# A hybrid decoder block on one core: six shared temporary tiles for the attention stage, the gate's sigmoid in place, forget gate and token sums by turns, attention heads stored by ScalarE

## The chip, the cores and the metric

The kernel runs on one core of a Trainium2 chip. A core has five engines, and each works through a queue of instructions of its own in program order: TensorE (PE, matrix products, with its weight loads listed apart as PEld), VectorE (DVE), ScalarE (ACT), GpSimd (POOL) and SyncE (SP). SP computes nothing; most transfers between device memory and the on-chip memory are issued from its queue, some from POOL's, and after the change some from ScalarE's. Engines wait for each other and for transfers by semaphores. The metric is the device time of one launch in microseconds (us), as the median of several runs. The kernel is written with a layer that tracks which tile is written and read by whom, and that places the waits.

## The reference

One layer of a decoder for 512 tokens of width 2048, all in float32. The token mixer has two groups of heads behind one input projection; both outputs are concatenated and go through one output projection `w_o`. A gated feed-forward stage with a short convolution follows. Cut to the stage that the change touches:

```python
proj = h @ w_in            # columns: gq, gk, gv, gg, ga, dq, dk, dv
log_a = log_sigmoid(ga @ w_alpha_up + b_alpha) / GLA_TAU          # forget gate, rank 16
o_a = gla_chunked(gq, gk, gv, log_a)                              # 4 heads, 128 keys, 256 values
o_a = rmsnorm(o_a, gla_norm) * silu(gg)                           # silu(g) = g * sigmoid(g)
lam = exp(sum(lambda_q1 * lambda_k1)) - exp(sum(lambda_q2 * lambda_k2)) + lambda_init
# diff_attention, 4 heads, causal, in query blocks of 128:
p = softmax(q k^T * scale + alibi)                                # for two halves, p1 and p2
o_b = rmsnorm((p1 - lam * p2) @ v, diff_norm) * (1 - lambda_init)
m = concatenate([o_a, o_b]) @ w_o
x = x + rmsnorm(m, attn_post_norm)
# then the feed-forward part
```

## The kernel before

**Products in halves.** Every float32 operand of a large product is split into a rounded high part and the rest: ScalarE copies the high part (L137 for weights, L150 for activations), VectorE subtracts it (L138, L151), and PE makes three products, high by high, low by high, high by low. The split weights go through a ring of three slots (`ring`), so PE can be two slots behind the splits and no more. The activations lie in `ah` and `al` for the whole stage.

**The input projection in units.** Most of the 6,160 columns of `w_in` are done in units of 512 columns (class `InUnit`), each by seven block products instead of eight. The seven segments are called x0, z0, y0, z1, x1, y1 and y2; each has two ring slots of 24 products with 256 columns (L743 to L745). Four of them use sums of token blocks, `s5`, `s2`, `s3` and `s7`, which `first_sums` and `last_sums` make beforehand out of `ah` and `al` (VectorE L404 to L425, then split). A segment adds up in a bank of the product memory; a bank that is used for a second term must be copied out first (L754, L759, L768, L790 on ScalarE, L773, L779 and L784 on VectorE). So L759 copies z0's bank (tile `u11`), and z1, which runs with `s3` in the same bank, waits for that.

**Background work.** The attention itself is not a stage of its own. It is written as generators in a list `fill`; after each ring slot `step()` advances the first generator in the list by a share that `pace` sets. First come `forget_gate`, `first_sums` and `last_sums`, one after the other, under the first projections; then `gla_heads` and `diff_heads` under the units. The order of instructions in each engine's queue is then set by a list scheduler with a cost model, within the limits of the tiles and banks; the first 52 us, and some blocks far behind this stage, are placed by hand.

**What the generators do.** `forget_gate` loads the 16 columns of `ga` (tile `gar`), splits them into `gas` (columns 0 to 15 high, 64 to 79 low, zeros between), makes 32 products with 80 columns of weights by 512 tokens (L446, L447), copies the result (L449), makes four more products (L457) and takes -|z| through exp and ln in two wide tiles `za` of 1024 columns (L459 to L465), then a prefix sum (L470). `gla_head` does seven levels a head, each with a product (L522) that VectorE merges under a mask (L525) and with the factor tile `qe` (L513). `diff_heads` works in query blocks: two score products (L614), softmax (exp on ScalarE L622, scaling L629, difference on VectorE L630), four stages behind each other: the probabilities are turned by PE (L637) and copied (L639), multiplied with the values (L646), normalized (L649, L652), turned again (L659), copied into a `dst` tile (L661) and stored to device memory through SP's queue (L662, which the profile lists under the helper's line L48).

**The end of the stage.** The last two of ten units are those of the gate. As each quarter of a gate unit comes out, `done` loads the matching part of the GLA output (`op`), takes the sigmoid into a tile `sg` (L811), multiplies (L812, L813) and, for the first unit, stores to `ogd`. Then `place_diff` loads the stored heads (`dt`) and `turn_gate` loads `ogd` (`ogt`) and turns the blocks on PE (L825), so that `ah` and `al` hold the mixer's output, which `w_o` multiplies (L191 to L193).

**Tiles.** The stage's temporaries come from rings of buffers by tag: `tmp` (four of 2 KB a partition), `quarter` (three of 1 KB), `wide` (two of 4 KB), `qk` (four), `ub` (five). A ring hands out its buffers in turn, and a new tile waits until the last use of the one that had its buffer.

Of the kernel before, what the change touches and what calls it, by code (L numbers as in the profile page):

```python
# [9 lines left out]
F32 = mybir.dt.float32  # L10
# [25 lines left out]
def hybrid_layer(ctx: ExitStack, tc: tile.TileContext, x, attn_pre_norm, w_in, w_alpha_up, b_alpha,  # L36
# [112 lines left out]
    def split(hi, lo, src):  # L149
        act(hi, src, AF.Copy)  # L150
        tt(lo, src, hi.bitcast(F32), ALU.subtract)  # L151
# [195 lines left out]
    for li, hs in enumerate(LEVELS):  # L347
        nb = 64 // hs
        m = quarter("m")[:, :64]
# [13 lines left out]
    lp = quarter("lp").rearrange("p (a d) -> p a d", a=2)  # L363
# [9 lines left out]
    cols = few.tile([P, 4 + 4 * NF], F32, name="cols")  # L373
    rows = tmp("rows")[:NF, :].rearrange("p (a d) -> p a d", a=4)
    ba = quarter("ba")[:4, :P]
# [8 lines left out]
    nc.vector.tensor_copy(cols, cb[:, :4 + 4 * NF])  # L384
# [44 lines left out]
    def forget_gate():  # L429
        gar = quarter("gar").rearrange("p (k r) -> p k r", r=RANK)  # L430
        dma(gar, w_in3[:, :, C_GA:C_GA + RANK])
        gas = mx.tile([P, KT, 80], F32R, name="gas", tag="v", bufs=1)
        nc.gpsimd.memset(gas.bitcast(F32), 0.0)
        split(gas[:, :, 0:RANK], gas[:, :, 64:64 + RANK], gar)
        wup = block_tile("wup")[:80, :]
        nc.gpsimd.memset(wup, 0.0)
        dma(wup[0:RANK, :], w_alpha_up[0])
        dma(wup[64:64 + RANK, :], w_alpha_up[0])
# [5 lines left out]
        gav = gab[:80, :].rearrange("p (t c) -> p t c", c=P)  # L444
# [3 lines left out]
        gaT = block_tile("gaT")[:80, :]  # L448
        nc.vector.tensor_copy(gaT, gab[:80, :])  # L449
# [44 lines left out]
    def gla_head(h, q, k, b, got, fetch):  # L494
        e0 = (h % 2) * GDV
        room = mx.tile([P, NT * GDV + 256], F32, name="gvt", tag="v", bufs=1)
        vt, ec = room[:, :NT * GDV].rearrange("p (t e) -> p t e", t=NT), room[:, NT * GDV:NT * GDV + 4]
# [5 lines left out]
        def prepare(hs):  # L503
# [8 lines left out]
            qe = quarter("qe")  # L512
# [19 lines left out]
        nxt = prepare(LEVELS[0])  # L532
        yield
        for li, hs in enumerate(LEVELS):
            cur = nxt
            if li + 1 < len(LEVELS):
                nxt = prepare(LEVELS[li + 1])
# [20 lines left out]
        st = None  # L558
        for c in range(4):
# [12 lines left out]
            if c < 3:  # L572
                pk = bank()
                mm(pk[:, :GDV], kT[:, c * P:(c + 1) * P], vc, start=True, stop=True)
                ns = quarter("st")
# [10 lines left out]
    def diff_heads():  # L586
# [68 lines left out]
        def store(n, on):  # L655
# [6 lines left out]
            dma(dstd[h][:, :, qb * P:(qb + 1) * P], o.rearrange("p (j c) -> p j c", j=2))  # L662
# [33 lines left out]
    class InUnit:  # L696
        count = 0

        def __init__(self, turned, cols, done):
# [935 lines left out]
```

## Time and profile before

| | |
|---|---|
| median of 3 runs | 2121.33 us (2121.28 to 2121.49) |
| profiled execution | 2118.62 us, span 2116.9 us |
| busy in the span: PE / DVE / ACT / POOL | 2067.5 / 1535.6 / 981.3 / 283.3 us |
| transfers | 358.60 MB, mean 169 GB/s |
| granted TensorE clock, mean | 0.994 |

Times in the trace are counted from the start of the span. Up to 52 us the first projections run in an order by hand; the forget gate and the token sums lie between 52 and 160 us, the GLA heads from there to about 425 us and the attention heads from about 440 to 612 us; `w_o` starts in earnest at 640 us. PE is busy nearly throughout, so a change can win only where PE waits or where its clock is lowered, and lose wherever it makes PE wait. In lists of waits a row names the engine and line that waited, then who released it, then the total, the number of times and the longest. In rows of single instructions the bracket at the end gives the idle time of that engine ahead of the instruction and what ended it. In tables by stretch of time each engine has its busy time and its number of instructions; PEclk is the clock that was granted to TensorE, as a share of full speed.

### The profile page before, as it was taken

Reading aid. Unit: us, or ns where it says so; the run is one execution under the profiler, and the core shown is the slowest. Engines: PE = TensorE matmul, PEld = TensorE weight load, DVE = VectorE, ACT = ScalarE, POOL = GpSimd, SP = SyncE. Lnnn points to the kernel's source line nnn. Section 1 sums busy time; section 2 is a strip of 40 time slices with the busy share of each in tenths; the row PEclk is TensorE's granted clock in tenths of the full one; section 3 lists DMA queues with packets and bytes.
Section 4 is the critical chain, followed back from the end, with each engine's and each line's share of the span. In section 5 each row is a group of like instructions: output and inputs, shape, how many; then the busy total and the mean of one; then the engine's idle time right before and its main releaser. Section 6 shows DMA issues by size and latency. Waiting matters only on the chain.

```text
span 2116.9 us, 35567 instructions
## 1 busy us (share of the span) xinstructions
PE 2067.5 (98%) x14449; PEld 1908.2 (90%) x14449; DVE 1535.6 (73%) x1844; ACT 981.3 (46%) x1264; POOL 283.3 (13%) x306
## 2 busy tenths in 40 slices
PE   7999999999979999999999999999999999999998
PEld 6789999999878889899999999999999878887886
DVE  5596776666763246887786777877877868888887
ACT  4454444455652234353544544454444554444443
POOL 0112222222200000001111111111110111110100
PEclk9999999999989999999999999999999999999999
DMA  5469878888754344457757667577567777676653
GB/s 208 144 151 199 196 167 186 180 198 201 170 179 169 100 157 161 120 120 172 172 129 192 151 145 192 141 174 175 140 164 186 212 230 180 173 195 168 168 168 141
DMA packets 280696, 358.60 MB, mean 169 GB/s; under 512 B 14592, under 2 KB 221876, under 8 KB 278612
## 3 DMA queue, kind: packets, MB, share of 16 engines
q1 hardware_dynamic: 195732, 261.95, 36.5%
q0 software_dynamic: 84800, 94.38, 29.3%
q8 instruction: 113, 1.85, 0.3%
q14 instruction: 51, 0.42, 0.1%
HBM read 311.72 MB, written 44.56 MB: 168 GB/s over the span
## 4 chain that ended last, share of the span: by engine, by line
PE 48%; issue 41%; POOL 3%; DVE 3%; DMA 3%; ACT 1%; POOLq 0%; SPq 0%; DVEq 0%; ACTq 0%
PE bank L192 3%; PE bank L193 3%; PE bank L191 3%; PE bank L739 3%; PE bank L741 3%; PE bank L740 3%; PE bank L743 3%; PE bank L745 3%; PE bank L744 3%; PE bank L1217 2%; PE bank L1216 2%; PE bank L1215 2%; PE bank L175 2%; PE bank L174 2%; PE bank L173 2%
## 5 line engine op out<-in xcount | busy, mean ns | idle before, releaser
L137 ACT ACTIVATE ring<-raw 128x1024 fp32r<-128x1024 f32 x315 | 333.2, 1060 | 523.8 <-PE bank L1216 113.1
L138 DVE TENSOR_TENSOR ring<-raw,ring 128x1024 fp32r<-128x1024 f32 x315 | 383.9, 1221 | 243.2 <-ACT ring L137 241.2
L1217 PE MATMUL bank<-ah,ring 128*128 128x256 f32 x1280 | 354.1, 277 | 1.7 <-DVE ring L138 1.7
L1215 PE MATMUL bank<-ah,ring 128*128 128x256 f32 x1280 | 353.4, 276 | 0.0
L1216 PE MATMUL bank<-al,ring 128*128 128x256 f32 x1280 | 353.4, 276 | 0.0
L137 ACT ACTIVATE ring<-rt 128x1024 fp32r<-128x1024 f32 x221 | 233.2, 1059 | 223.1 <-PE bank L1216 139.6
L138 DVE TENSOR_TENSOR ring<-rt,ring 128x1024 fp32r<-128x1024 f32 x221 | 269.0, 1221 | 89.4 <-ACT ring L137 87.3
L1217 PEld LDWEIGHTS bank<-ah,ring 128*128 128x128 f32 x1280 | 240.2, 188 | 3.0 <-DVE ring L138 3.0
L1215 PEld LDWEIGHTS bank<-ah,ring 128*128 128x128 f32 x1280 | 240.3, 188 | 0.1
L1216 PEld LDWEIGHTS bank<-al,ring 128*128 128x128 f32 x1280 | 240.2, 188 | 0.1
L1318 PE MATMUL bank<-ring,ah 128*128 128x512 f32 x424 | 166.5, 393 | 4.2 <-DVE ring L138 4.2
L1319 PE MATMUL bank<-ring,al 128*128 128x512 f32 x424 | 165.1, 389 | 0.0
L1317 PE MATMUL bank<-ring,ah 128*128 128x512 f32 x424 | 158.3, 391 | 1.5 <-ACT ring L137 1.0
L192 PE MATMUL bank<-ring,ah 128*128 128x512 f32 x280 | 109.8, 393 | 0.0
L191 PE MATMUL bank<-ring,ah 128*128 128x512 f32 x280 | 109.7, 396 | 0.1
L193 PE MATMUL bank<-ring,al 128*128 128x512 f32 x280 | 109.6, 394 | 0.0
L1163 POOL DMA_DIRECT2D raw<-in_w_ffn_in_dram x40 | 50.9, 1274 | 406.5 <-DVE ring L138 403.5
L1318 PEld LDWEIGHTS bank<-ring,ah 128*128 128x128 f32 x424 | 79.6, 188 | 24.8 <-DVE ring L138 8.7
L743 PE MATMUL bank<-ring,ah 128*128 128x256 f32 x320 | 93.6, 293 | 4.3 <-DVE u L784 1.9
L1317 PEld LDWEIGHTS bank<-ring,ah 128*128 128x128 f32 x424 | 79.4, 188 | 20.0 <-ACT ring L137 3.0
L1319 PEld LDWEIGHTS bank<-ring,al 128*128 128x128 f32 x424 | 79.6, 188 | 16.3
L1163 POOL DMA_DIRECT2D rt<-in_w_ffn_in_dram x40 | 51.0, 1280 | 321.1 <-DVE ring L138 242.9
(349 smaller groups left out, 5691.1 us busy)
## 6 DMA issues: line engine op xcount, KB each, us to landing
raw<-in_w_ffn_in_dram SPq DMA_DIRECT2D x96, 512.0 KB, 5.9
raw<-in_w_in_dram SPq DMA_DIRECT2D x56, 512.0 KB, 5.2
raw<-in_w_ffn_out_dram SPq DMA_DIRECT2D x48, 512.0 KB, 6.4
raw<-in_w_in_dram POOLq DMA_DIRECT2D x40, 512.0 KB, 6.8
rt<-in_w_ffn_in_dram SPq DMA_DIRECT2D x40, 512.0 KB, 6.2
rt<-in_w_ffn_in_dram POOLq DMA_DIRECT2D x40, 512.0 KB, 6.0
raw<-in_w_ffn_in_dram POOLq DMA_DIRECT2D x40, 512.0 KB, 7.3
raw<-in_w_o_dram SPq DMA_DIRECT2D x32, 512.0 KB, 3.7
```

The lines of the kernel that those rows point to most:

```text
L137: act(hi, raw, AF.Copy)
L138: tt(lo, raw, hi.bitcast(F32), ALU.subtract)
L191: mm(banks[t], ah[:, t, s, :], w[0][:, k, :], start=st, stop=False)
L192: mm(banks[t], ah[:, t, s, :], w[1][:, k, :], start=False, stop=False)
L193: mm(banks[t], al[:, t, s, :], w[0][:, k, :], start=False, stop=sp)
L743: mm(o, sh[:, n, kk, :], wh[:, k, :], start=st, stop=False, **NOW)
L1215: mm(o, wh, sh[:, :, kk, :], start=start and kk == 0 and n == 0, stop=False, **NOW)
L1216: mm(o, wh, sl[:, :, kk, :], start=False, stop=False, **NOW)
L1217: mm(o, wl, sh[:, :, kk, :], start=False, stop=kk == HK - 1, **NOW)
L1317: mm(b[j], sh[:, o:o + P], w[0][:, q, :], start=start and st == 0, stop=False, **NOW)
L1318: mm(b[j], sh[:, o:o + P], w[1][:, q, :], start=False, stop=False, **NOW)
L1319: mm(b[j], sl[:, o:o + P], w[0][:, q, :], start=False, stop=st == 3, **NOW)
```

## The change

Six things are changed at once.

- The ring `tmp` grows from four to six buffers, and the ring `quarter` goes; what used it (mask `m`, `lp`, `ba`, `gar`) takes a `tmp` tile. In a GLA head `qe` now alternates between the two halves of one `tmp` tile, so it has two buffers instead of three, and the state `st` does the same. The on-chip memory used stays the same.
- `gas` has 48 columns instead of 80, the low part at 32.
- `za` is four `qk` tiles of 512 columns instead of two wide ones; exp and ln run on four tiles, with a pause of the generator between them. The wide tiles are then free for the token sums.
- `forget_gate` and the token sums are advanced by turns instead of one after the other.
- In a gate unit a hook `before` loads `op` ahead of the last segment of a quarter; `done` multiplies `op` by u first (VectorE), takes the sigmoid in place on u (ScalarE), and multiplies. There is no tile `sg`.
- The 16 stores of `dst` are issued by ScalarE's queue.

```diff
     def tmp(name):
-        return mx.tile([P, S], F32, name=name, tag="tmp", bufs=4)
-
-    def quarter(name):
-        return mx.tile([P, 256], F32, name=name, tag="w1", bufs=3)
...
-        m = quarter("m")[:, :64]
+        m = tmp("m")[:, :64]
...
-    lp = quarter("lp").rearrange("p (a d) -> p a d", a=2)
+    lp = tmp("lp")[:, :256].rearrange("p (a d) -> p a d", a=2)
...
+    ec = cols[:, 4 + 4 * NF:]
     rows = tmp("rows")[:NF, :].rearrange("p (a d) -> p a d", a=4)
-    ba = quarter("ba")[:4, :P]
+    ba = tmp("ba")[:4, :P]
...
     def forget_gate():
-        gar = quarter("gar").rearrange("p (k r) -> p k r", r=RANK)
+        gar = tmp("gar")[:, :KT * RANK].rearrange("p (k r) -> p k r", r=RANK)
         dma(gar, w_in3[:, :, C_GA:C_GA + RANK])
-        gas = mx.tile([P, KT, 80], F32R, name="gas", tag="v", bufs=1)
+        gas = mx.tile([P, KT, 48], F32R, name="gas", tag="v", bufs=1)
         nc.gpsimd.memset(gas.bitcast(F32), 0.0)
-        split(gas[:, :, 0:RANK], gas[:, :, 64:64 + RANK], gar)
-        wup = block_tile("wup")[:80, :]
+        split(gas[:, :, 0:RANK], gas[:, :, 32:32 + RANK], gar)
+        wup = block_tile("wup")[:48, :]
...
-        zs = [wide("za") for _ in range(2)]
-        za, bt = [z[:, h * S:(h + 1) * S] for z in zs for h in range(2)], []
+        za, bt = [], []
         for h in range(GH):
             zb = bank()
             mm(zb, wup[:, h * P:(h + 1) * P], gaT, start=True, stop=True)
             bcol = cols[:, h:h + 1]
+            za.append(qk_tile("za"))
             bt.append(tmp("bt"))
             act(za[h], zb, AF.Abs, bias=bcol)
             ts(bt[h], zb, bcol, 0.0, ALU.add, ALU.min)
             if h % 2:
                 yield
-        for z in zs:
+        for z in za:
             act(z, z, AF.Exp, scale=-1.0)
-        for z in zs:
+        yield
+        for z in za:
             act(z, z, AF.Ln, bias=1.0)
         yield
         for h, m in enumerate(za):
...
+        pairs = [tmp("qe"), None]
+
+        def prepare(li, hs):
...
-            qe = quarter("qe")
+            qe = pairs[0][:, 256 * (li % 2):256 * (li % 2 + 1)]
...
-            dma(dstd[h][:, :, qb * P:(qb + 1) * P], o.rearrange("p (j c) -> p j c", j=2))
+            nc.scalar.dma_start(out=dstd[h][:, :, qb * P:(qb + 1) * P], in_=o.rearrange("p (j c) -> p j c", j=2))
...
+            last = {"z1": (1, 0), "x1": (0, 0), "y1": (1, 1), "y2": (0, 1)}
+            if self.before and seg in last:
+                self.before(*last[seg])
...
     def gate_unit(c):
+        heads = {}
+
+        def before(j, i):
+            op = heads[j, i] = tmp("op")
+            dma(two(op), oad[2 * c + j][:, 2 * i:2 * i + 2, :])
+
         def done(j, i, u):
-            op, sg = tmp("op"), tmp("sg")
-            dma(two(op), oad[2 * c + j][:, 2 * i:2 * i + 2, :])
-            act(sg, u, AF.Sigmoid)
-            tt(u, u, sg, ALU.mult)
+            op = heads.pop((j, i))
+            tt(op, op, u, ALU.mult)
+            act(u, u, AF.Sigmoid)
             tt(u, u, op, ALU.mult)
             if c == 0:
                 dma(ogd[:, 2 * i:2 * i + 2, 256 * j:256 * (j + 1)], two(u))
             else:
                 kept_u[j, i] = u
 
-        return InUnit(False, (C_GG + 512 * c, C_GG + 512 * c + 256), done)
+        return InUnit(False, (C_GG + 512 * c, C_GG + 512 * c + 256), done, before)
...
+    def in_turn(*gens):
+        gens = list(gens)
+        while gens:
+            for g in list(gens):
+                try:
+                    next(g)
+                except StopIteration:
+                    gens.remove(g)
+                    continue
+                yield
+
+    def token_sums_in():
+        yield from first_sums()
+        yield from last_sums()
+
+    fill.append(in_turn(forget_gate(), token_sums_in()))
     pace[0] = 1.6
```

What that moves is seen in the queues. First VectorE at the start of the stage (from about 52 us). Before; `q` and `r` are token sums, `gaT` the result of the forget gate's products, `bt` and `za` its exp and ln part, `ring<-raw` the splits of weights:

```order
L353 CAST masks_432<-m_458 128x256
...
L138 TENSOR_TENSOR ring_84<-raw_706,ring_84 128x1024
...
L151 TENSOR_TENSOR gas_530<-gar_528,gas_530 128x16x16
...
L449 COPY gaT_602<-bank_569 80x512
L460 TENSOR_SCALAR bt_608<-bank_606,cols_485 128x512
...
L470 SCALAR_TENSOR_TENSOR bt_613<-keep_538,za_604 128x512
L138 TENSOR_TENSOR ring_84<-raw_816,ring_84 128x1024
L404 TENSOR_TENSOR q_740<-ah_79 128x1024
...
L151 TENSOR_TENSOR in_s5l_427<-q_740,in_s5h_426 128x1024
...
L151 TENSOR_TENSOR in_s2l_429<-q_740,in_s2h_428 128x1024
```

After:

```order
L402 TENSOR_TENSOR q_569<-ah_79 128x1024
...
L403 TENSOR_TENSOR q_569<-q_569,al_80 128x1024
...
L404 TENSOR_TENSOR q_569<-q_569,al_80 128x1024
...
L138 TENSOR_TENSOR ring_84<-raw_642,ring_84 128x1024
L138 TENSOR_TENSOR ring_84<-raw_702,ring_84 128x1024
L151 TENSOR_TENSOR in_s5l_427<-q_569,in_s5h_426 128x1024
...
L151 TENSOR_TENSOR gas_530<-gar_528,gas_530 128x16x16
...
L151 TENSOR_TENSOR in_s2l_429<-q_569,in_s2h_428 128x1024
...
L447 COPY gaT_608<-bank_575 48x512
...
L458 TENSOR_SCALAR bt_685<-bank_682,cols_485 128x512
```

The token sums, which stood behind the forget gate's prefix sums, now stand ahead of the forget gate's split (`gas`) and are split into `s5` and `s2` before `gaT` is copied.

Next ScalarE at the end of the stage. Before; `s` are the scores of a query block (the softmax passes of a block are two L622 and one L629), `u` and `p` are quarters of a gate unit, and `dst` a turned block:

```order
L649 ACTIVATE jk_5877,ss_5876<-bank_5874 128x256
L629 ACTIVATE s_5822<-s_5822,r2_5832 128x256
...
L639 ACTIVATE aT_5888<-bank_5885 128x256
L661 ACTIVATE dst_5988<-bank_5985 128x256
L811 ACT_TABLE_LOAD
L811 ACTIVATE sg_5948<-u10_5840 128x512
...
L622 ACT_TABLE_LOAD
L622 ACTIVATE s_5892,l_5898<-s_5892,nm_5896 128x384
L622 ACTIVATE s_5904,l_5910<-s_5904,nm_5908 128x384
...
L629 ACTIVATE s_5904<-s_5904,r2_5914 128x384
L759 ACTIVATE u11_6358<-bank_6305 128x512
L639 ACTIVATE aT_6007<-bank_6003 128x384
```

After:

```order
L622 ACTIVATE s_5784,l_5790<-s_5784,nm_5788 128x256
L662 DMA dstd2_416<-dst_5847 256x1x128
L622 ACTIVATE s_5796,l_5802<-s_5796,nm_5800 128x256
...
L820 ACT_TABLE_LOAD
L820 ACTIVATE u10_5814<-u10_5814 128x512
L629 ACTIVATE s_5796<-s_5796,r2_5806 128x256
...
L762 ACTIVATE u11_6328<-bank_6275 128x512
...
L622 ACTIVATE s_5868,l_5874<-s_5868,nm_5872 128x384
L820 ACT_TABLE_LOAD
L820 ACTIVATE p1_5526<-p1_5526 128x512
L622 ACT_TABLE_LOAD
...
L629 ACTIVATE s_5880<-s_5880,r2_5890 128x384
```

The first sigmoid with its table load, and the store of a block, now stand between a block's exps and its scaling L629; in the next block a second sigmoid stands between the two exps, with a load on either side of it; and the copy of `u11` has moved from behind that block's L629 to ahead of its exps.

Last PE at the same place. Before; L743 to L745 are the products of a gate unit, `in_s3h` those of segment z1, which adds into the bank that L759 empties, and bank_6503 that of x1:

```order
L646 MATMUL bank_5991<-dvt_5836,aT_5888 128x256 x2
...
L745 MATMUL bank_6503<-ring_84,ah_79 128x256
L743 MATMUL bank_6305<-ring_84,in_s3h_430 128x256
...
L637 MATMUL bank_6003<-ident_70,s_5892 128x128 x3
L614 MATMUL bank_6009<-dk_5638,dq_5636 128x512
...
L659 MATMUL bank_6063<-ident_70,on_6001 128x128 x2
...
L743 MATMUL bank_6503<-ring_84,ah_79 128x256
...
L637 MATMUL bank_6082<-ident_70,s_6011 128x128 x4
L659 MATMUL bank_6149<-ident_70,on_6080 128x128 x2
L646 MATMUL bank_6155<-dvt_5836,aT_6087 128x256 x4
...
L743 MATMUL bank_6181<-ring_84,ah_79 128x256
...
L825 MATMUL bank_6565<-ident_70,ogt_6563 128x128 x4
```

After (bank_6275 is now z1's, bank_6474 x1's, bank_6152 that of y1 and y2, bank_6749 and bank_6750 are those of `w_o`):

```order
L746 MATMUL bank_6275<-ring_84,in_s3h_430 128x256
...
L637 MATMUL bank_5978<-ident_70,s_5868 128x128 x3
L614 MATMUL bank_5984<-dk_5612,dq_5610 128x512
...
L659 MATMUL bank_6038<-ident_70,on_5976 128x128 x2
...
L646 MATMUL bank_6044<-dvt_5810,aT_5982 128x256 x3
...
L746 MATMUL bank_6152<-ring_84,ah_79 128x256
...
L191 MATMUL bank_6749<-ring_84,ah_79 128x512
...
L637 MATMUL bank_6057<-ident_70,s_5986 128x128 x4
...
L192 MATMUL bank_6749<-ring_84,ah_79 128x512
...
L646 MATMUL bank_6129<-dvt_5810,aT_6062 128x256 x4
...
L659 MATMUL bank_6179<-ident_70,on_6141 128x128 x2
L833 MATMUL bank_6533<-ident_70,ogt_6531 128x128 x4
```

All but six of z1's products now stand ahead of the turning of the second last block (L637 x3, where 21 stood before), and the last block's turn (L637 x4), its values (L646 x4) and its last turn (L659) have moved from ahead of y1 to behind y1 and y2, among the first products of `w_o`, and the turning of the gate (L833, which was L825) with them.

More of the change, by code (lines that the diff above doesn't have):

```diff
@@ L336, in tmp @@
     def tmp(name):
-        return mx.tile([P, S], F32, name=name, tag="tmp", bufs=4)
-    def quarter(name):
-        return mx.tile([P, 256], F32, name=name, tag="w1", bufs=3)
+        return mx.tile([P, S], F32, name=name, tag="tmp", bufs=6)
     def row_tile(name):
@@ L557, in gla_head @@
         yield
-        st = None
+        st, pairs[1] = None, tmp("st")
         for c in range(4):
@@ L574, in gla_head @@
                 mm(pk[:, :GDV], kT[:, c * P:(c + 1) * P], vc, start=True, stop=True)
-                ns = quarter("st")
+                ns = pairs[1][:, 256 * (c % 2):256 * (c % 2 + 1)]
                 if c == 0:
```

25 lines of the change are left out of this document (11 added, 14 removed).

## Prediction

> **What bounds the kernel now.** I read the page first, for the share of each engine; then the table by stretch of time, for where PE is not busy or not at full clock; then the list of PE's waits in those stretches; and last single rows, for what stands in the queue of whoever releases PE.
>
> ```profile
> span 2116.9 us, 35567 instructions
> PE 2067.5 (98%) x14449; PEld 1908.2 (90%) x14449; DVE 1535.6 (73%) x1844; ACT 981.3 (46%) x1264; POOL 283.3 (13%) x306
> ```
>
> PE carries the kernel: it idles 2116.9 - 2067.5 = 49.4 us in all. What the change touches ends at about 640 us, so the question is how much of PE's loss lies there. The stretches of that stage:
>
> ```profile
> core 0: us, PE busy (x) PEld busy (x) DVE busy (x) ACT busy (x) POOL busy (x), PEclk, DMA share, GB/s
> 50.00:90.00 40.00, 40.00 (x177) 30.34 (x176) 17.39 (x36) 17.30 (x22) 6.69 (x18) 1.00 0.40 112
> 130.00:160.00 30.00, 27.17 (x232) 26.77 (x232) 30.00 (x52) 16.57 (x22) 5.05 (x4) 1.00 0.87 191
> 160.00:570.00 410.00, 408.63 (x3369) 399.48 (x3369) 283.29 (x464) 202.23 (x335) 99.19 (x111) 1.00 0.83 187
> 570.00:632.00 62.00, 48.49 (x298) 43.62 (x297) 40.94 (x71) 37.29 (x68) 5.99 (x10) 0.86 0.64 183
> ```
>
> Between 50 and 90 us PE has no gap and VectorE is free for more than half of the time; between 130 and 160 us VectorE is full and PE loses 2.8 us; in 410 us of heads PE loses 1.4 us; and in the 62 us at the end it loses 13.5 us, at a clock of 0.86. The waits of the last and of the second of these four stretches:
>
> ```profile
> PE bank L743 <- ACT u L759: 4.4, 1, 4.4
> PE bank L659 <- DVE on L652: 2.8, 1, 2.8
> PE bank L637 <- DVE s L630: 2.7, 2, 2.2
> PE bank L743 <- DVE u L784: 1.9, 1, 1.9
> PE bank L743 <- ACT u L768: 1.2, 1, 1.2
> ...
> PE bank L745 <- DVE ring L138: 1.6, 1, 1.6
> PE bank L743 <- ACT ring L137: 1.2, 1, 1.2
> ```
>
> What a lowered clock costs shows behind the longest wait:
>
> ```profile
> 584.15 0.58 PE L743 MATMUL bank<-ring,in_s3h 128*128 128x256 f32 x1 [4.42 <-ACT u L759]
> 584.53 0.41 PE L744 MATMUL bank<-ring,in_s3l 128*128 128x256 f32 x1
> 584.75 0.41 PE L745 MATMUL bank<-ring,in_s3h 128*128 128x256 f32 x1
> ...
> 587.99 0.28 PE L744 MATMUL bank<-ring,in_s3l 128*128 128x256 f32 x1
> 588.11 0.28 PE L745 MATMUL bank<-ring,in_s3h 128*128 128x256 f32 x1
> ...
> 584.00:588.00 4.00, 3.85 (x20) 3.85 (x21) 0.90 (x2) 0.10 (x1) 0.00 (x0) 0.57 0.40 131
> 608.00:614.00 6.00, 4.82 (x23) 4.50 (x22) 3.28 (x5) 2.02 (x4) 0.00 (x0) 0.50 0.80 255
> ```
>
> Products stand 0.22 us apart at first (584.53, 584.75) and 0.12 at the end. Some 15 slow ones at 0.095 more cost 1.4 us; by the stretch's row, 4.00 x 0.43 = 1.7. The clock is also low from 608 to 614 us, behind waits of 2.8 and 1.2. Over the whole end it loses at most 62 x 0.14 = 8.7 us, and over PE's busy time 48.5 x 0.14 = 6.8; I take 7.5. The end of the stage thus loses 13.5 + 7.5 = 21.0 us, and it is from here that the change can take much.
>
> **The change part by part, the end of the stage.** The 4.42 us first. These rows of ScalarE show why the copy of `u11` (L759) was late:
>
> ```profile
> 577.26 1.28 ACT L811 ACT_TABLE_LOAD   x1 [0.53 <-PE bank L646]
> 578.56 0.63 ACT L811 ACTIVATE sg<-u 128x512 f32<-128x512 f32 x1
> ...
> 579.57 1.28 ACT L622 ACT_TABLE_LOAD   x1
> 580.87 0.61 ACT L622 ACTIVATE s<-s,nm 128x384 f32<-128x384 f32 x1
> ...
> 582.08 1.04 ACT L137 ACTIVATE ring<-raw 128x1024 fp32r<-128x1024 f32 x1
> 583.02 0.60 ACT L629 ACTIVATE s<-s,r 128x384 f32<-128x384 f32 x1
> 583.53 0.57 ACT L759 ACTIVATE u<-bank 128x512 f32<-128x512 f32 x1
> ```
>
> Two loads, a sigmoid, two exps, a weight split and a scaling stood ahead of it. In the new order it stands right behind the copy of a `dst` tile, ahead of both exps, and should be done at about 580 us, while PE needs its bank some 21 products after the block's L646, at about 582. This wait goes, and so does the clock's dip behind it. The other four at the end of y1 and y2 (2.8, 2.2, 1.9 and 1.2) belong to a block that no longer stands there: PE has y1 and y2 to do while that block is made.
>
> What is late instead, walked through ScalarE's new queue:
>
> ```profile
> 574.12 0.44 PE L637 MATMUL bank<-ident,s 128*128 128x128 f32 x2 [0.49 <-DVE s L630]
> 576.35 0.38 ACT L661 ACTIVATE dst<-bank 128x256 f32<-128x256 f32 x1 [1.38 <-PE bank L659]
> 614.92 0.60 PE L825 MATMUL bank<-ident,ogt 128*128 128x128 f32 x4
> ...
> L48 SPq DMA_DIRECT2D dstd<-dst x16: 513/525/645, 450.3 to 610.3; - x16
> DMA to landing us min/median/max: 2.1/4.9/6.4
> ...
> L48 SPq DMA_DIRECT2D dt<-dstd x8: 517/570/610, 589.6 to 619.0; - x8
> L48 SPq DMA_DIRECT2D ogt<-ogd x4: 371/442/553, 608.8 to 620.2; - x4
> DMA to landing us min/median/max: 4.5/4.5/4.5
> ```
>
> - L637 x2 waited 0.49. Ahead of the scaling that releases it now stand the store's issue (0.525, if ScalarE takes as long for it as SP), a table load (1.28) and the sigmoid (0.63): 0.49 + 2.44 = 2.9.
> - L637 x3 did not wait (the list has two waits of that line, 0.49 and 2.2). PE comes to it after 576.6 + 2.8 (the scores and values between, as now) + 63 products x 0.12 = 587, and some 0.5 later for the clock. ScalarE goes from the `dst` copy, now at about 579.1, through u11 0.57, store 0.525, the rest of L649 0.6, load, exp 0.8, load, sigmoid 0.63, load, exp 0.8, split 1.06, scaling 0.6, which with three loads of 1.28 makes 9.4; VectorE's L630 (0.6) and the hand-overs bring it to 589.5. Wait: 2.2.
> - The backlog reaches the weight splits: one of y1 and the first of `w_o` come late, by 0.8 and 1.0 in my walk. The nearest rows are the 1.6 and 1.2 above; bounds 0 and 2.8, and I take 1.8, since by then ScalarE has only copies and splits ahead.
> - The last block's store goes last. From its turn (L659): copy 0.38, some 0.9 until ScalarE issues, 0.525, landing 4.9, then on SP's queue `dt` 0.57, `ogt` 0.44, landing 4.5: 12.2. PE has 25 products of `w_o` at 0.227 and four turnings at some 0.6 to do in it, with what overlaps 8.5 to 9.4: wait 3.0 (0, if the store lands in 2.1 as the fastest did, to 4.5 at 6.4).
>
> New waits: 2.9 + 2.2 + 1.8 + 3.0 = 9.9. Three are over 2 us, and I charge each 1.43 of clock: 14.2 against 21.0. The end gains 6.8, say 7.0. Of VectorE's products each quarter has two before and two now, and the eight sigmoids cost the same; loading `op` ahead takes nothing off PE's path but what the list above has.
>
> The Trainium skill, "TensorE: Matmul & The Clock Gate", Part 1, says that the clock falls after an idle window of about 3.4 us and comes back after as long a busy one. The row of 4.42 us agrees, and 3.4 us is what the slow products last there; the 0.50 behind waits of 2.8 and 1.2 does not agree with one idle window. By the page's rule none of my new waits would lower the clock, and the end would gain 21.0 - 9.9 = 11.1; I keep to the rows.
>
> **The start of the stage.**
>
> ```profile
> 66.02 0.42 ACT L150 ACTIVATE gas<-gar 128x256 fp32r<-128x256 f32 x1 [2.78 <-DMA gar<-in_w_in_dram]
> 68.09 0.40 PE L446 MATMUL bank<-ah,gas 128*80 128x512 f32 x1
> 91.34 1.22 DVE L404 TENSOR_TENSOR q<-ah 128x1024 f32<-128x1024 f32 x1
> ```
>
> The sums start at 91 us now, and VectorE is full by 130; that makes the 1.6 and 1.2. By turns they start at about 55 us in idle time of VectorE and are over some 20 us sooner: those 2.8 us go (with the edges 3.1). Against it, `lt` now takes a `tmp` tile that a mask must have left, and `gar` is queued on SP behind it: I put the split of `gas` some 3 us later than its 66.02, and the first product on it at 70.4 instead of 68.09, so PE waits about 2.3. Net gain 0.8; bounds: a gain of 3.1 (if PE has other products to go on with) and a loss of 2, if the lag is 5. The 32 products on `gas` have 512 columns as before, so the narrower weights save nothing; the smaller exp tiles and two more table loads fall where ScalarE is busy 17 of 40 us.
>
> **The middle.** 16 stores at 0.525 are 8.4 us more for ScalarE, which is busy 202 of 410 us there, and PE's 1.4 of waiting has nothing to do with it. Without that cover each would delay a scaling by 0.525. For `qe` with two buffers I read from the new order that each L513 stands right behind an L525 of VectorE that already waits for the product that frees the buffer: nothing.
>
> The sum: 7.0 + 0.8 + 0 = 7.8 us less. On the profiled execution's 2118.62 that is 2110.8; the median, 2.71 above it, gives 2113.5.
>
> **Rivals.** *All of it.* If the late waits stay short of lowering the clock but for one, and the last store lands as the fastest did, the end loses 9.9 - 3.0 + 1.4 = 8.3 and gains 12.7; with the start 2107.8. The store's spread of 2.1 to 6.4 speaks for it as much as against.
>
> *Little of it.* ScalarE becomes the pace of the end: five table loads there instead of three, and four stores. If my walk is short by a queue place here and there, L637 x2 and x3 and the last chain each wait 1.0 to 1.5 longer and one more dip of the clock follows: 14.2 + 3.8 + 1.4 = 19.4, a gain of 1.6, with the start 2118.9. For it speaks that ScalarE is busy 37 of 62 us there already.
>
> The Trainium skill, "ScalarE: Activation LUTs", What ACT_TABLE_LOAD costs, gives a load of some 1283 ns and a drain of 1380 ns. The load agrees with 1.28 us here, but 577.26 + 1.28 is followed by an activation at 578.56, 0.02 us on, so the rows show no drain. By the page's figures four loads in the two chains would cost 5.5 more, an estimate that leaves 7.8 - 5.5 = 2.3 and 2119.0, this same rival.
>
> *Slower.* The two buffers of `qe`:
>
> ```profile
> L525 DVE COPY_PREDICATED sc<-masks,bank x28: 414/450/742, 148.1 to 395.5; 128x256 f32<-128x256 uint8 x28
> ```
>
> 28 levels, seven in each head. If VectorE, waiting for a buffer, holds back the weight splits behind it and PE waits with it, it costs 28 times that wait; from 7.8 / 28 = 0.28 us each it cancels the gain, and at 0.5 it gives 2113.5 + 14 = 2127.5. Against it: VectorE idles 127 of 410 us there, and PE never waited for a split in that stretch.
>
> **How the numbers follow.** A measurement of this kernel can tell about 0.2%, 4.2 us: faster is under 2117.1, slower over 2125.6. The forecast (2109 to 2117) has 0.57, all of it 0.13, little of it 0.17, slower 0.07, and 0.06 is left for a later `gas` or another misplacement at the start that eats the gain (about 2121). Faster: 0.57 + 0.13 and a third of the third, 0.76; slower 0.08; the rest 0.16. The range takes in both neighbours, 2107.8 and 2118.9, with what the landing's spread adds: 2105 to 2121.
>
> **What would show it.** In the changed kernel PE's list at the end should have no wait for the copy of `u11`; two waits of L637 for L630, of 2 to 3 us; and one of L833 for `ogt`. No wait for a split between 130 and 160 us, and one of about 2 for `gas` near 68. The heads should show no new wait. The prediction is wrong if PE waits for splits in the heads, if the waits for L630 are 4 us and over, or if the start slips by more than 3.

## The result, and the profile after

Over 16 runs the changed kernel takes 2112.28 us in the median, the kernel before, run beside it, 2124.2. The ratio is 0.9943 (95% interval 0.9931 to 0.9955): 0.57% faster, or 12.1 us on the 2121.33 of the first three runs. One run of each kernel was far slower (2581.48 and 7406.96 us) and is not in the ratio. The forecast was 7.8 us less, 2113.5. The profiled execution of the changed kernel took 2113.65 us, only 5.0 less than the 2118.62 of before; why the profiles differ by less than the medians is told below.

The page of the changed kernel, its stretches by time, and PE's waits (the first two rows at the start of the stage, the third between the groups of heads, the last three at its end; `issue` means that the profile shows nothing that PE waited for):

```profile
span 2111.9 us, 35519 instructions
...
PE 2064.1 (98%) x14449; PEld 1900.7 (90%) x14449; DVE 1536.5 (73%) x1844; ACT 988.4 (47%) x1272; POOL 286.6 (14%) x306
```

```profile
50.00:90.00 40.00, 37.20 (x159) 25.69 (x156) 37.86 (x52) 18.75 (x24) 10.65 (x18) 1.00 0.38 112
130.00:160.00 30.00, 30.00 (x252) 29.61 (x251) 19.23 (x31) 16.65 (x21) 6.32 (x5) 1.00 0.85 186
160.00:570.00 410.00, 407.97 (x3364) 398.75 (x3363) 286.19 (x473) 201.91 (x336) 96.23 (x109) 1.00 0.83 185
570.00:632.00 62.00, 54.02 (x342) 47.99 (x341) 40.24 (x73) 38.87 (x67) 7.21 (x10) 0.94 0.67 182
```

```profile
PE bank L379 <- issue: 1.7, 1, 1.7
PE bank L444 <- DVE gas L151: 1.1, 1, 1.1
...
PE bank L614 <- DMA dk<-dkd: 2.0, 1, 2.0
...
PE bank L637 <- DVE s L630: 5.8, 2, 3.7
PE bank L191 <- ACT ring L137: 1.8, 1, 1.8
PE bank L746 <- DVE u L787: 0.2, 1, 0.2
```

Against the rows of before: at the end PE idles 8.0 us instead of 13.5, and the clock is 0.94 instead of 0.86. The wait for `u11` is gone, and so are the four of the last block. At the start it is the other way round: VectorE, which was busy 17.4 of the 40 us, is now full (37.86), the two waits for splits behind 130 us are gone, and PE has two new ones, 2.8 us together.

How far one kernel leads the other is read at the same instruction in both. Two such marks are used throughout: the square of the thirteenth block of the attention heads (L649), which stands ahead of the end, and the first copy of `w_o`'s result. Before, then after:

```profile
572.24 0.36 ACT L649 ACTIVATE jk<-bank 128x256 f32<-128x256 f32 x1
...
670.05 0.60 ACT L921 ACTIVATE m<-bank 128x512 f32<-128x512 f32 x1 [0.30 <-PE bank L193]
```

```profile
573.52 0.36 ACT L649 ACTIVATE jk<-bank 128x256 f32<-128x256 f32 x1
...
661.58 0.60 ACT L944 ACTIVATE m<-bank 128x512 f32<-128x512 f32 x1 [0.30 <-PE bank L193]
```

Up to the first the changed kernel is 1.3 us late. From the first to the second it needs 88.06 us instead of 97.81: the end gains 9.75. At the second it leads by 8.5. What follows has the same instructions in the same order, so the rest is scatter: in the twelve profiles of this study the last 430 us of the kernel (from the first copy of `acc` in the last part, L1346 in the changed kernel, to ScalarE's last square, L1562) take 426.5 to 437.6, and before's profile has the lowest of these, the changed kernel's 433.4. That is how a lead of 8.5 became 5.0 in this pair.

What PE waits for at the end, on ScalarE (then the two rows of PE):

```profile
573.99 1.28 ACT L820 ACT_TABLE_LOAD   x1
575.29 0.63 ACT L820 ACTIVATE u<-u 128x512 f32<-128x512 f32 x1
...
581.94 0.60 ACT L762 ACTIVATE u<-bank 128x512 f32<-128x512 f32 x1 [2.18 <-DMA ogd<-u]
...
583.16 1.28 ACT L622 ACT_TABLE_LOAD   x1
...
586.48 0.64 ACT L820 ACTIVATE p<-p 128x512 f32<-128x512 f32 x1
...
577.09 0.44 PE L637 MATMUL bank<-ident,s 128*128 128x128 f32 x2 [2.18 <-DVE s L630]
591.29 0.55 PE L637 MATMUL bank<-ident,s 128*128 128x128 f32 x3 [3.65 <-DVE s L630]
```

The copy of `u11` is early in the queue, as forecast, but it sits there for 2.18 us until a store to `ogd` has read the buffer that it writes, and all behind it on ScalarE is late by as much.

### The profile page after: what moved, and what is told of

Its sections match the earlier page's. It is cut to its first block, busy times and chain, and to the rows that moved or that the text cites. A ratio compares the mean times of both kernels' runs of the same rounds, so it can differ in the third digit from the quotient of the medians.

```text
span 2111.9 us, 35519 instructions
## 1 busy us (share of the span) xinstructions
PE 2064.1 (98%) x14449; PEld 1900.7 (90%) x14449; DVE 1536.5 (73%) x1844; ACT 988.4 (47%) x1272; POOL 286.6 (14%) x306
## 4 chain that ended last, share of the span: by engine, by line
issue 51%; PE 37%; POOL 4%; DVE 3%; DMA 3%; ACT 1%; POOLq 0%; SPq 0%; DVEq 0%; ACTq 0%
PE bank L192 3%; PE bank L193 3%; PE bank L742 3%; PE bank L191 3%; PE bank L744 3%; PE bank L743 3%; PE bank L746 3%; PE bank L747 3%; PE bank L748 3%; POOL rt L1186 2%; POOL raw L1186 2%; PE bank L522 1%; DVE ring L138 1%; PE bank L614 1%; PE bank L646 1%
```

## The experiments

The theory: the gain is the new order at the end of the stage, that order comes from the gate's part alone, and the other parts only shift a few us. The rivals: the larger ring, or the stores on ScalarE, make the gain. "Start" is the time of the thirteenth block's square less that of before (572.24), "end" the time from there to the first copy of `w_o`, both of one profile; the ratio is to the kernel before on the same chip.

| kernel | median us | ratio (95%) | start | end us |
|---|---|---|---|---|
| before | | | 0 | 97.81 |
| changed | 2112.28 | 0.9943 (0.9931 to 0.9955) | +1.3 | 88.06 |
| gate alone | 2117.37 | 0.9959 (0.9945 to 0.9972) | +0.4 | 91.14 |
| stores alone | 2128.15 | 1.0016 (1.0004 to 1.0028) | +1.1 | 101.13 |
| changed, old gate | 2122.36 | 0.9991 (0.9977 to 1.0006) | +1.1 | 94.04 |
| changed, wide za | 2111.66 | 0.9937 (0.9920 to 0.9954) | -2.0 | 86.23 |
| gate and stores | 2114.77 | 0.9943 (0.9923 to 0.9963) | +3.1 | 87.45 |
| changed, six ub | 2115.36 | 0.9951 (0.9934 to 0.9968) | +5.3 | 86.20 |
| changed, masks later | 2113.75 | 0.9944 (0.9922 to 0.9965) | +3.7 | 86.92 |
| changed, sigmoid by exp | 2128.65 | 1.0013 (1.0001 to 1.0026) | +0.4 | 101.22 |
| wide za and six ub | 2111.99 | 0.9929 (0.9912 to 0.9946) | +0.6 | 88.42 |
| changed, once more | 2115.58 | 0.9945 (0.9928 to 0.9961) | +1.2 | 88.17 |

Between the two marks PE has 452 products in every kernel. Four of the kernels (changed, wide za, masks later, changed once more) have there the same instructions in the same order on PE, ScalarE, VectorE and GpSimd, and their ends are 88.06, 86.23, 86.92 and 88.17. So one profile's end can't tell less than 2 us.

**The gate alone.**

```diff
 # the kernel before, with the changed kernel's run() hook and gate_unit
-            op, sg = tmp("op"), tmp("sg")
-            act(sg, u, AF.Sigmoid)
+            op = heads.pop((j, i))
+            tt(op, op, u, ALU.mult)
+            act(u, u, AF.Sigmoid)
```

> The kernel before with the gate part alone: the hook that loads op early, the sigmoid in place, no sg tile; four tmp buffers, quarter tiles, wide za, no turns, stores on SP. Theory (the whole gain is the new order at the end of the stage, and that comes from the gate): the order of PE and ScalarE there is nearly that of the changed kernel, so the end gains 9 to 10 us as in the changed kernel (from 1.3 behind to 8.5 ahead), no wait for u11, two waits of L637 of about 2 and 3.5 us; the start is as before, so about 10 us less than before, ratio 0.9953. Rival (the tmp ring or the stores make the gain): within 2 us of before.

It is 0.41% faster, and the end gains 6.7 us. PE's waits in it at the end:

```profile
PE bank L637 <- DVE s L630: 5.9, 2, 4.3
PE bank L191 <- ACT ring L137: 2.7, 1, 2.7
PE bank L833 <- DMA ogt<-ogd: 2.4, 2, 1.5
```

The wait for `u11` is gone and the two of L637 are there, with the same sum as in the changed kernel (5.9 against 5.8) but not the same shares: 4.3 at L637 x2, where the sigmoid stands idle for 1.36 us until VectorE has multiplied `op`, and 1.5 at x3, where the copy of `u11` finds its buffer free. The order at the end comes from the gate; which of its two parts, the load ahead or the sigmoid in place, does it, no run separates. The end gains 3 us less than in the changed kernel, and the wait for `ogt` that the prediction had put into the changed kernel is here.

**The stores alone.**

```diff
 # the kernel before
-            dma(dstd[h][:, :, qb * P:(qb + 1) * P], o.rearrange("p (j c) -> p j c", j=2))
+            nc.scalar.dma_start(out=dstd[h][:, :, qb * P:(qb + 1) * P], in_=o.rearrange("p (j c) -> p j c", j=2))
```

> The kernel before with the 16 dst stores on ScalarE's queue and nothing else; no other instruction moves in any queue. Theory: 0.52 us more of ScalarE for each store is hidden in the heads; at the end each of the last three blocks delays ScalarE by 0.5, at most 1.5 us in all, so within -1 and +2 us of before. Rival (stores on SP hold back the loads behind them, and moving them is where the gain comes from): 5 us or more faster.

It is 0.16% slower, more than was expected; the start loses 1.1 and the end 3.3.

```profile
PE bank L743 <- ACT u L759: 5.3, 1, 5.3
PE bank L637 <- DVE s L630: 3.5, 2, 3.0
PE bank L825 <- DVE al L151: 3.5, 1, 3.5
```

The first two waits were 4.4 and 2.7, and the third is new. The larger first wait fits ScalarE, whose queue releases PE there and now holds the stores as well. The third is not the stores alone: from about 615 us on the queues differ from before's, against the expectation (the scheduler has put the gate's turnings L825 and the copies for them in other places). The stores by themselves are no gain.

**Without the gate's part.**

```diff
 # the changed kernel, with the gate_unit of before
-            op = heads.pop((j, i))
-            tt(op, op, u, ALU.mult)
-            act(u, u, AF.Sigmoid)
+            op, sg = tmp("op"), tmp("sg")
+            act(sg, u, AF.Sigmoid)
```

> The changed kernel with the gate part of before: op loaded when the quarter is done, sg tile, sigmoid out of place. Theory: the end of the stage has the order and the waits of before again (4.4 for the copy of u11, 2 to 3 for the last block), some 11 to 13.5 us of idle, and the kernel is as slow as before, within 2 us. Rival: it keeps more than half of the gain, 2115 or less where before is at 2122.

The gain is lost: the ratio is 0.9991 and its interval holds 1. In its profile the end is still 3.8 us shorter than before's. The wait for `u11` is back.

```profile
PE bank L637 <- DVE s L630: 4.7, 2, 4.2
PE bank L746 <- ACT u L762: 4.2, 1, 4.2
PE bank L746 <- ACT u L771: 2.7, 1, 2.7
```

**Gate and stores together.**

```diff
 # the gate-alone kernel, and
-            dma(dstd[h][:, :, qb * P:(qb + 1) * P], o.rearrange("p (j c) -> p j c", j=2))
+            nc.scalar.dma_start(out=dstd[h][:, :, qb * P:(qb + 1) * P], in_=o.rearrange("p (j c) -> p j c", j=2))
```

> The kernel before with two parts, the gate and the stores on ScalarE's queue. With the gate alone the end gained 6.7 us (in the profiles, from the last normalization before it to the first copy of the output projection's banks), with two waits of L833 for ogt (2.4 us) that the changed kernel does not have. Theory (those two waits come from the last stores of the heads waiting in SP's queue, and ScalarE's queue takes them out of it): no wait for ogt, the end gains 9 to 10 as in the changed kernel, 3 us faster than the gate alone. Rival (the stores do nothing but cost ScalarE time, as they did alone, 0.16% slower): the same as the gate alone or up to 3 us slower.

```profile
PE bank L637 <- DVE s L630: 3.6, 2, 2.4
...
PE bank L833 <- DMA ogt<-ogd: 0.9, 1, 0.9
```

The ratio is the changed kernel's, 0.9943, and the end gains 10.4, 3.7 more than with the gate alone; the intervals of the two ratios overlap. The waits for `ogt` fall from 2.4 to 0.9, not to nothing, and the rows do not put them down to SP's queue. In the gate-alone kernel (the last turn on PE, the copy, the store, the load behind it):

```profile
625.91 0.38 PE L659 MATMUL bank<-ident,on 128*128 128x128 f32 x2
631.08 0.37 ACT L661 ACTIVATE dst<-bank 128x256 f32<-128x256 f32 x1
631.48 0.57 SPq L48 DMA_DIRECT2D dstd<-dst  x1
633.64 0.57 SPq L48 DMA_DIRECT2D dt<-dstd  x1
```

SP sends the store out as soon as the copy is done, and the load follows 2.2 us later. What is late is the copy, 5.2 us behind its turn, since it stands on ScalarE behind sigmoids that wait for `op`; with the stores on ScalarE it is 4.0 behind (626.47, 630.42), and in the changed kernel 0.4 (629.14, 629.56). So the theory's queue is not the cause, and how much of the 3.7 us the stores make stays open. The larger ring, the narrower `gas`, the small `za` and the turns add nothing that these runs can tell.

**The start: za in wide tiles.**

```diff
 # the changed kernel
-            za.append(qk_tile("za"))
+        zs = [wide("za") for _ in range(2)]
+        za, bt = [z[:, h * S:(h + 1) * S] for z in zs for h in range(2)], []
```

> The changed kernel with za in two wide tiles again. In the queues the token sums then go one after the other and the second one ends later; the loads of lt, ba and gar stay as late as in the changed kernel. Theory (the lateness at the start, 1.7 us ahead of L379 and 1.1 ahead of L444, comes from lt taking a tmp tile behind the masks, and the lead of the sums only makes up for it): the 2.8 us at 65 to 71 us stay, and part of the 2.8 us of waits for splits at 137 to 155 us comes back: 0 to 3 us slower than the changed kernel. Rival (four za tiles cause the lateness): the waits near 65 us go.

Here the theory fell and the rival held: PE has no wait between 50 us and the heads, and the start is 3.3 us ahead of the changed kernel's. The loads of `lt`, `ba` and `gar` are as late as there (`ba` goes out at 61.08 us, in the changed kernel at 61.58), but with one wide tile for the sums at a time VectorE comes to the split of `gas` sooner (69.19 instead of 70.92), and PE's queue takes up `ba` 13 products later:

```profile
66.27 0.22 PE L379 MATMUL bank<-ident,ba 4*128 4x4 f32 x1
...
69.68 0.41 PE L444 MATMUL bank<-ah,gas 128*48 128x512 f32 x1
```

Why the loads are late is seen in part on GpSimd. The selections that make the masks, before and after:

```profile
54.46 0.66 POOL L351 TENSOR_SCALAR_AFFINE_SELECT m<-m 128x64 f32<-128x64 f32 x3
```

```profile
53.96 4.56 POOL L348 TENSOR_SCALAR_AFFINE_SELECT m<-m 128x64 f32<-128x64 f32 x6
```

0.22 us each before, 0.76 in the mean after, when VectorE makes the token sums at the same time: in the trace the three of the six that lie beside a sum take 1.23 to 1.28 us, the others 0.24 to 0.31. `lt` waits for the masks' buffers and goes out at 59.71 instead of 52.76. Of these 7 us the slower selections make some 3 (an estimate: six times 0.54); the rest is that `lt` now waits for a mask at all. The Trainium skill, "GPSIMD Engine Reference", in its table of specifications, says that GpSimd shares its memory interface with VectorE and contends with instructions of two inputs from that memory; the sums are such instructions, and the two rows agree with it.

**The masks later.**

```diff
 # the changed kernel: the loop over the masks becomes a generator
+    def make_masks():
+        for li, hs in enumerate(LEVELS):
...
-    fill.append(in_turn(forget_gate(), token_sums_in()))
+    fill.append(in_turn(forget_gate(), token_sums_in(), make_masks()))
```

> The changed kernel with the seven masks made by a background generator behind the forget gate's split instead of ahead of everything, so that lt, ba, rows and gar take tmp buffers that nobody holds. Theory (the two waits of PE at the start, 1.7 at L379 and 1.1 at L444, come from loads queued behind lt, which waits for a mask; the masks are late because GpSimd's selections take 0.76 us each while VectorE makes the sums, and 0.22 when it does not): these loads go out at 53 us as before, both waits are gone, about 2.5 us faster than the changed kernel up to the first head. Rival (the split of gas waits in VectorE's queue behind the sums, not for its load): the waits stay.

Both waits are gone and `ba` goes out at 58.59, but nothing is gained, since another wait takes their place:

```profile
PE bank L173 <- ACT gv L858: 2.6, 1, 2.6
```

PE comes 1.6 us sooner to the projections behind (L173), and the copy of the bank that it needs comes 2.1 later on ScalarE (79.33 instead of 77.20), behind a split of token sums that waits for VectorE; a window at half clock follows. For the wait at L379 the cause is shown: with `ba` loaded earlier it is gone. For the one at L444 the rival held as much: the high part of `gas` is ready at 64.54 here and at 66.72 in the changed kernel, and the low part stands in VectorE's queue for over 4 us in both (69.19, 70.92). What bounds the start is VectorE.

**A sixth buffer for the units' tiles.**

```diff
 # the changed kernel
-        return mx.tile([P, 512], F32, name=name, tag="ub", bufs=5)
+        return mx.tile([P, 512], F32, name=name, tag="ub", bufs=6)
-        return mx.tile([P, S], F32, name=name, tag="tmp", bufs=6)
+        return mx.tile([P, S], F32, name=name, tag="tmp", bufs=5)
```

> The changed kernel with six ub buffers and five tmp buffers, the same memory. In the changed kernel the copy of u11 (L762) waits 2.18 us for the buffer that a store to ogd still reads, and everything behind it on ScalarE is late with it; PE's wait of 3.65 at L637 x3 follows. Theory: the copy goes out earlier without waiting, L637 x3 waits 1.5 instead of 3.7, 2 us faster than the changed kernel, 4 with a dip of the clock less. Rival (the three table loads alone set that wait, or the fifth tmp buffer is missed): no faster.

```profile
572.52 0.58 ACT L762 ACTIVATE u<-bank 128x512 f32<-128x512 f32 x1
```

The copy of `u11` goes out without a wait and PE's waits of L637 are both gone. But the run does not isolate the buffer: the copy now starts 9 us earlier, ahead of work of the sixth block that it stood behind in ScalarE's queue, and PE comes to L637 x3 behind two waits for weight splits (2.4 and 0.8). The end takes 86.20 us, 1.9 less than in the changed kernel and no less than with the wide `za` (86.23), where `u11` waits 2.09. The start, whose order changes too, is 5.3 behind before, and the ratio is no better than the changed kernel's. So neither the mechanism nor a gain is shown by this run; what the wait for the buffer costs is read from rows in the next section.

**The sigmoid without its table.**

```diff
 # the changed kernel
-            act(u, u, AF.Sigmoid)
+            act(u, u, AF.Exp, scale=-1.0)
+            ts(u, u, 1.0, None, ALU.add)
+            nc.vector.reciprocal(u, u)
```

> The changed kernel with the sigmoid as 1 / (1 + exp(-u)): exp on ScalarE, the sum and the reciprocal on VectorE, so that the end of the stage has no change of tables; two more VectorE passes for each of eight quarters. Theory (table loads ahead of L629 make the two waits of L637): the wait at L637 x2 falls from 2.2 to about 0.9, the one at L637 x3 from 3.7 to about 1.1 or less, 3 to 4 us faster than the changed kernel if VectorE has room. Rival (VectorE becomes the pace at the end, a reciprocal of 128x512 takes several times 0.6 us): new waits for VectorE, no faster or slower.

```profile
L822 DVE RECIPROCAL u<-u 128x512 f32<-128x512 f32 x6 | 20.0, 3339 | 0.0
```

The rival held: a reciprocal of this size takes 3.34 us of VectorE, eight of them 26.7, and PE waits for VectorE and ScalarE instead; 0.13% slower than before. The waits at L637 do shrink to 0.7 in all, but the order changes with the edit, and PE waits for the copy of `u11` again (3.9).

**Both edits that helped a stage, and the changed kernel once more.** Wide `za` and six `ub` buffers together, beside the changed kernel on the same chip:

```diff
 # the changed kernel
-            za.append(qk_tile("za"))
+        zs = [wide("za") for _ in range(2)]
...
-        return mx.tile([P, 512], F32, name=name, tag="ub", bufs=5)
+        return mx.tile([P, 512], F32, name=name, tag="ub", bufs=6)
-        return mx.tile([P, S], F32, name=name, tag="tmp", bufs=6)
+        return mx.tile([P, S], F32, name=name, tag="tmp", bufs=5)
```

> The changed kernel with both edits that helped a stage: za in two wide tiles, and six ub with five tmp buffers. In the profiles the wide za put the start 3.3 us ahead of the changed kernel (2.0 ahead of the kernel before instead of 1.3 behind), and the sixth ub buffer gained 11.6 us at the end instead of 9.7. Theory (the two stages are independent): no wait at L379 or L444, no wait of L637's kind, 4 to 5 us faster than the changed kernel, ratio to the kernel before 0.992. Rival (what the start wins is scatter from run to run, as its waits differ among kernels with the same order): 2 us faster at most, 0.9935 or more.

> The changed kernel once more, on the chip and beside the runs of the kernel with wide za and six ub buffers. Ratio 0.9943 as measured first. In its profile the wait for u11's buffer and the waits at L637 come back at the same size (2.2 and 3.7 within 0.5); the waits at the start (1.7 and 1.1) within 1 us; the dips of the clock may differ in number, since a dip depends on where a wait falls in windows of 3.4 us.

The first has the lowest ratio of all, 0.9929, against 0.9945 for the changed kernel beside it. The step is 0.16% (3.6 us in the medians) and the intervals overlap, so it is not shown that it beats the changed kernel. Its profile, of an execution 7 us above its median (2118.90), does not bear out that the stages add up. Waits of PE in the stage, of the kernel with both edits and then of the changed one:

```profile
PE bank L745 <- ACT ring L137: 2.8, 1, 2.8
PE bank L745 <- DVE u L786: 2.5, 1, 2.5
PE bank L444 <- DVE gas L151: 2.2, 1, 2.2
```

```profile
PE bank L637 <- DVE s L630: 4.4, 2, 2.2
...
PE bank L444 <- DVE gas L151: 1.1, 1, 1.1
```

No wait of L637's kind is left, but other ones stand in the same place, and `gas` is waited for again at the start. In the changed kernel, with every instruction in the same order, the waits at the start come back within 0.3 us. At the end the expectation missed: the wait for the buffer of `u11` is 0.85 instead of 2.18, and the wait of 3.65 is one of 2.25. The release comes at the same time (591.18 against 591.29); PE is 1.3 later, behind a window at half clock that the first profile does not have.

## Why the prediction was right, and where its steps were off

- **The direction and the place.** Right: the end gains, the heads do not change (2.0 instead of 1.4 us of waiting), and the gate's part decides, as the run with the gate alone and the run without it show.
- **What goes.** Right: the 4.42 for `u11` and the four waits of the last block are not there. The 2 us to spare that the walk gave `u11` (done at 580, needed at 582) were not: the copy ends at 582.54 and PE uses the bank at 582.60. Before's loss was taken as 21.0; the record of the granted clock gives 13.5 of waiting and 17.1 us at half speed, 22.0.
- **L637 x2**, taken as 2.9, measured 2.18 in both profiles. The issue of a store, 0.52 in its row, ran beside the activation ahead of it and cost ScalarE next to nothing there. Behind a short copy it does cost: ScalarE is idle for 0.60 at the store of 617.20.
- **L637 x3**, taken as 2.2 (its own figures, 589.5 and 587.5, give 2.0), measured 3.65 and 2.25. PE came when the walk said, at 587.6; the release was late. The walk had `u11` copied at once; it waits 2.18 for its buffer. From the copy of `dst` ahead of it to the scaling L629 ScalarE takes 10.60 us (579.38, 589.98); in the gate-alone kernel and the one with gate and stores, where `u11` waits for nothing, the same stretch takes 8.58 and 8.51. So the wait for the buffer comes through in full, and that step of the walk was wrong.
- **Weight splits**, taken as 0.8 and 1.0: one wait of 1.84, at the first of `w_o`; the one in y1 did not come.
- **`ogt`**, taken as 3.0: none. These are the last rows of that chain, the store from ScalarE's queue, then SP's:

```profile
630.06 0.52 ACTq L662 DMA_DIRECT2D dstd<-dst  x1
...
632.19 0.53 SPq L48 DMA_DIRECT2D dt<-dstd  x1
632.81 1.06 SPq L48 DMA_DIRECT2D ogt<-ogd  x2
```

The load follows the store after 2.1 us, the fast end of the landings and not the median of 4.9 that the sum took. With the stores in SP's queue the last one is as fast; the wait there (2.4) comes from the late copy.

- **The clock**, taken as three dips of 1.43, had two, which cost 3.4, and three in the second profile. In all the end was to lose 14.2 and lost 8.0 + 3.4 = 11.4, which against 22.0 is a gain of 10.6. The rows above give 9.75, and the 0.9 between is not explained; the forecast was 7.0.
- **The start**, taken as a gain of 0.8, lost 0.5 up to the GLA heads (1.3 with the later wait for `dk`). The waits for splits went as said (2.8 of the 3.1 credited). The lag came out in its size, 1.7 + 1.1 against 2.3, but only in part on the prediction's path: 1.7 is at `ba`, and `gar` was hardly late. The high part of `gas` is made 0.7 later than before (66.72, 66.02); its low part then stands behind token sums in VectorE's queue until 70.92 (66.47 before). The sum had no term for VectorE, which is full between 50 and 90 us. Where the last 0.5 goes is not shown.
- **Little of it** and **slower** did not come, though L637 x3 was 1.5 longer in the first profile, as the former had it. No wait for `qe` is seen (VectorE is idle for 0.3 us ahead of L513 in all the heads). Loads of tables ahead of a scaling do set a wait, but the row of the sigmoid follows the load's end by 0.02 us (573.99 + 1.28, 575.29), as before: no drain.

So the mechanism of the end was right and its total near, since the terms missed to both sides: `u11`'s buffer cost more, the last store and the clock less. Of the time itself part is luck: 2112.28 lies 1.2 from the forecast of 2113.5, but the kernel before took 2124.2 beside it and not 2121.33, and the gain is 12.1 and not 7.8.

The profiles lead by 8.5 us at the output projection, and the ratio says 12.1 with an interval of 9.5 to 14.6. Where the rest lies isn't settled: no later stage differs in its instructions, and their scatter is as large as the difference.

## What to carry to other kernels

When a scheduler sets the order, a small edit that frees an instruction of its inputs (here `op` loaded ahead, the sigmoid in place) can move a whole block of work behind other work, and that is worth more than the instructions saved: read what stands ahead of the releaser in its queue, not only how long it takes. A copy that is early in the queue is not early if its buffer isn't free, so ask for each moved write who last read the buffer. And what a transfer costs in the queue of an engine depends on the order around it: the stores on ScalarE lost 0.16% with before's gate, and nothing that these runs can tell with the new one.

## What the runs showed of the hardware

The granted clock goes by fixed windows of 3.41 us. Within a run all drops begin on one grid of that step, and a drop ahead of the kernel's end lasts one window or two. These are windows of the changed kernel, and then two of the gate-alone kernel:

```profile
589.14:592.56 3.42, 1.27 (x6) 0.79 (x7) 1.46 (x4) 3.25 (x5) 0.00 (x0) 1.00 0.11 37
592.56:595.97 3.41, 3.41 (x12) 2.27 (x11) 2.65 (x5) 0.40 (x2) 0.00 (x0) 0.50 0.36 101
606.21:609.62 3.41, 1.55 (x9) 1.11 (x9) 3.16 (x5) 1.56 (x2) 0.00 (x0) 1.00 0.94 319
609.62:613.03 3.41, 3.41 (x19) 3.41 (x18) 2.24 (x4) 1.76 (x3) 0.00 (x0) 0.50 0.60 165
```

```profile
602.97:606.38 3.41, 1.77 (x16) 1.57 (x14) 2.76 (x5) 2.34 (x6) 0.00 (x0) 1.00 0.91 257
606.38:609.79 3.41, 2.13 (x14) 1.70 (x15) 3.03 (x4) 1.55 (x4) 0.00 (x0) 1.00 0.82 281
```

PE idle for 2.15 and 1.86 us of a window is followed by a window at half clock; idle for 1.64 it is not. Over the twelve profiles, between 50 and 660 us, every full-speed window with 1.86 or more idle was followed by one at half speed, and none with 1.72 or less; between, at 1.76 to 1.80, it went both ways. So about half a window is enough. A wait of 2.2 us costs another 1.7 (half of 3.41, an estimate) or nothing, depending on where it falls in the grid: the 2.18 at L637 x2 left 1.61 idle in one window of the changed kernel, without a drop, and in its second profile all of it lay in one window, and a drop followed. The rule that the prediction weighed, from the Trainium skill, "TensorE: Matmul & The Clock Gate", Part 1, that it takes an idle window of some 3.4 us, does not hold here.
